# Row moves for the scan tables: three matmuls per pair of blocks, or three transfers and a mask

## The chip, the cores and the metric

The kernel runs on one core of one Trainium2 chip, in float32 arithmetic (TensorE works on numbers split into two parts). The metric is the device time of one execution in microseconds, lower is better, as a median of several runs.

## The reference

The program is a decoder trunk of two layers over 256 positions of width 2048. Layer 0 has a Mamba-2 branch and an attention branch in parallel, layer 1 is an S5 mixer, a diagonal complex state-space scan. The part that matters here is layer 1's scan:

```python
def s5_ssm(u, lam_re, lam_im, log_dt, b_re, b_im, c_re, c_im, d_skip):
    lam = lax.complex(lam_re, lam_im)                 # 128 groups x 64 states
    dt = jnp.exp(log_dt)[:, None]
    lam_bar = jnp.exp(lam * dt)
    b_bar = ((lam_bar - 1.0) / lam)[..., None] * lax.complex(b_re, b_im)
    c_mat = lax.complex(c_re, c_im)
    ...
        bu = jnp.einsum('gnm,blgm->blgn', b_bar, u_blk)
        ...
        _, hs = lax.associative_scan(_linear_recurrence, (a, bu), axis=1)
        y = jnp.einsum('gmn,blgn->blgm', c_mat, hs).real
    ...
    return y + d_skip * u

def reference(x, ...):
    for layer in range(2):
        h = ssd_moba_mixer(x, ...) if layer % 2 == 0 else s5_mixer(x, ...)
        x = layer_norm(alpha * x + h, ln_g[layer], ln_b[layer])
    return x
```

`s5_mixer` projects its input, runs `s5_ssm`, applies GELU and a GLU with a gate, and projects back.

## The kernel before

**The stream of weights.** All large products read weights in units of 128 partitions x 1024 float32 (512 KB). `split_to` loads a unit on SP's queue into one of four `raw` buffers, ScalarE rounds it to `wh` (L244) and VectorE takes the rest, `wl = raw - wh` (L249). `wh` and `wl` have four buffers each in the pool `st`. While TensorE works on one unit, `split_to(unit + 3)` has been written ahead. A product unit on TensorE is 12 matmuls of 512 columns: two halves of the unit, two row blocks of the output, and three terms (high x high, high x low, low x high; `xmm`, L293). `product_wide` orders the same work with the weights as the stationary side (L348, L349).

**Side work.** Everything else is written as small jobs. `pump` runs one or more of them after each unit: `jobs` are urgent, `back` is spread evenly up to a goal. `run` holds a job's instructions on ScalarE, VectorE and SP behind the splits of a unit two ahead. It does not hold POOL or TensorE.

**The order on each engine.** The program is built with `schedule_with_timeline_sim=True`: a planner decides, when the kernel is built, in which order each engine gets its instructions, from the times at which it expects their inputs to be ready. The code's order breaks ties. On the chip each engine then runs its own list strictly in that order and waits where an input isn't there. `tc.issue_after(x)` puts an instruction behind `x` on its engine.

**The tables of the S5 scan.** Layer 1 does its scan in steps of four positions, with tables for 16 blocks of eight groups each. The tables depend on the parameters alone, so they are made during layer 0, in the attention part, as `back` jobs, and stored in DRAM (`wb`, 1792 columns per block). Layer 1 loads them later (`wt`, L1273). For each block `block_jobs` makes:

- `bars` (L721), `efs`, `fcs`: factors on VectorE;
- `pes` (L765), once for each pair of an even and an odd block: four transposes for each block, stored with ScalarE's queue; 32 small matmuls (L780) whose result plus the skip term is `kt`, 128 rows x 128 columns (L782, L783). The rows come in groups of four, one group for each of 32 (group, channel) combinations, and the row inside a group is the lag;
- `mts` (L785), the step of the change, one job after the next block's `bars`: `om` gets four versions of `kt`. In version 3 - t the rows are moved up by t inside their group of four, and rows that would come from the next group are zero. Before the change, three matmuls with constant shift matrices (`shift`) do this on TensorE (L790), ScalarE copies each result out of PSUM (L794), and `om` is stored in two transfers on ScalarE's queue (L796).

After each block comes `phasors` (L695): 28 small operations on POOL and a store on POOL's own queue (L711). `phasor_job` holds it behind the last L934 written so far, POOL's one step of the attention part's rotary embedding; the transposes on TensorE need L934.

Of the kernel before, what the change touches and what calls it, by code (L numbers as in the profile page):

```python
# [9 lines left out]
F32 = mybir.dt.float32  # L10
# [38 lines left out]
def _fields(table, spec):  # L49
    at = 0  # L50
    for name, n in spec:
# [2 lines left out]
    return at  # L54


NCONST = _fields(CONST, [("ident", 128), ("causal", 256), ("tril", 128), ("shift", 384),
                         ("kmask", 16), ("sgn", 2), ("rope", 128), ("sel", 32)])
NPARAM = _fields(PARAM, [("convw", 96), ("convb", 24), ("normg", 16), ("ln0g", 16), ("ln0b", 16),
                         ("ssdd", 32), ("dtb", 1), ("alog", 1), ("s5d", 64)])  # L60
# [2 lines left out]
def _constants():  # L63
    c = np.zeros((P, NCONST), np.float32)

    def put(name, a):
        lo, hi = CONST[name]
        c[: a.shape[0], lo:hi] = a.reshape(a.shape[0], -1)

    i = np.arange(P)  # L70
    put("ident", np.eye(P, dtype=np.float32))
    causal = np.zeros((P, 256), np.float32)
    causal[:, 128:] = np.where(i[None, :] <= i[:, None], 0.0, NEG)
    put("causal", causal)
    put("tril", (i[None, :] >= i[:, None]).astype(np.float32))
    sh = np.zeros((P, 3, P), np.float32)
    for t in range(1, 4):
        for r in range(P):
            if r % 4 + t < 4:
                sh[r + t, t - 1, r] = 1.0  # L80
    put("shift", sh)
    put("kmask", ((i[:, None] % 4 == 3) & ((i[:, None] // 4) % 16 == np.arange(16)[None, :])).astype(np.float32))
    sg = np.where(i < 64, -1.0, 1.0).astype(np.float32)
    put("sgn", np.stack([sg, -sg], 1))
    inv = np.float32(500000.0) ** (-(np.arange(16, dtype=np.float32) * np.float32(2.0) / np.float32(32)))
    ang = np.arange(S, dtype=np.float32)[:, None] * inv[None, :].astype(np.float32)
    cos, sin = np.cos(ang).astype(np.float32).T, np.sin(ang).astype(np.float32).T
    put("rope", np.concatenate([cos, cos, -sin, sin], 0).T.reshape(2, P, 64).transpose(1, 0, 2))
    put("sel", np.tile(np.eye(32, dtype=np.float32), (2, 1)))
    return c  # L90
# [80 lines left out]
def trunk(tc, io, out):  # L171
# [8 lines left out]
    with ExitStack() as top:  # L180
# [274 lines left out]
        with ExitStack() as l0:  # L455
# [239 lines left out]
            def phasors(b):  # L695
# [14 lines left out]
                    n *= 2  # L710
                nc.gpsimd.dma_start(wb[b][:, 1280:1792].rearrange("p (a n) -> p a n", a=2), cs.rearrange("p a q c -> p a (q c)"))  # L711

            ktp = [None]
            pend = []
            late = []

            def block_jobs(b):
                h = {}
                gs = slice(8 * b, 8 * b + 8)

                def bars():  # L721
                    bc = h["bc"] = pp.tile([P, 4, 8, 16], F32, tag="bc", name=nm("bc"))
                    nc.sync.dma_start(bc.rearrange("p a g m -> p (a g m)"), io["s5bc"][b].rearrange("p a g m -> p (a g m)"))
                    bb = h["bb"] = pp.tile([P, 2, 8, 16], F32, tag="bb", name=nm("bb"))
                    cv = h["cv"] = pp.tile([P, 8, 16], F32, tag="cv", bufs=2, name=nm("cv"))
                    tm = pp.tile([P, 512], F32, tag="tm", name=nm("tm"))
                    tv = tm.rearrange("p (a g m) -> p a g m", a=4, g=8)
                    wr = wri[:, 0, gs].unsqueeze(2).to_broadcast([P, 8, 16])
                    wi = wri[:, 1, gs].unsqueeze(2).to_broadcast([P, 8, 16])
                    V.tensor_tensor(bb[:, 0], bc[:, 0], wr, op=OP.mult)  # L730
                    V.tensor_tensor(tv[:, 0], bc[:, 1], wi, op=OP.mult)
                    V.scalar_tensor_tensor(bb[:, 1], bc[:, 1], sgn, wr, op0=OP.mult, op1=OP.mult)
                    V.scalar_tensor_tensor(tv[:, 1], bc[:, 0], sgn, wi, op0=OP.mult, op1=OP.mult)
                    V.tensor_tensor(bb[:, 0], bb[:, 0], tv[:, 0], op=OP.add)
                    V.tensor_tensor(bb[:, 1], bb[:, 1], tv[:, 1], op=OP.subtract)
                    V.tensor_scalar(cv, bc[:, 2], nsg, None, op0=OP.mult)

                def lk(i, k):
                    return lam[:, i, gs, k - 1].unsqueeze(2).to_broadcast([P, 8, 16])

                def fk(i):
                    return lap[:, i, 4 * b : 4 * b + 4, :].unsqueeze(2).to_broadcast([P, 4, 16, 4])

                def efs():
                    bc, bb = h["bc"], h["bb"]
                    et = h["et"] = pp.tile([P, 8, 16, 4], F32, tag="et", bufs=2, name=nm("et"))
                    tm = pp.tile([P, 8, 16, 4], F32, tag="tm", name=nm("tm"))
                    for s in range(3):
                        V.tensor_tensor(et[:, :, :, s], bb[:, 0], lk(0, 3 - s), op=OP.mult)
                        V.tensor_tensor(tm[:, :, :, s], bb[:, 1], lk(1, 3 - s), op=OP.mult)  # L750
                    V.tensor_tensor(et[:, :, :, 0:3], et[:, :, :, 0:3], tm[:, :, :, 0:3], op=OP.add)
                    V.tensor_copy(et[:, :, :, 3], bb[:, 0])

                def fcs():
                    bc = h["bc"]
                    ob = h["ob"] = pp.tile([P, 1024], F32, tag="ob", bufs=2, name=nm("ob"))
                    cp = [bc[:, 3, 4 * i : 4 * i + 4, :].unsqueeze(3).to_broadcast([P, 4, 16, 4]) for i in range(2)]
                    for r in range(2):
                        fv = ob[:, 512 + 256 * r : 768 + 256 * r].rearrange("p (g m t) -> p g m t", g=4, m=16)
                        tm = pp.tile([P, 4, 16, 4], F32, tag="tm", name=nm("tm"))  # L760
                        V.tensor_tensor(fv, cp[0], fk(r), op=OP.mult)
                        V.tensor_tensor(tm, cp[1], fk(1 - r), op=OP.mult)
                        V.tensor_tensor(fv, fv, tm, op=OP.add if r else OP.subtract)

                def pes():  # L765
                    pair = [(b - 1, pend.pop()), (b, h)]
                    pk = aux()
                    kt = ktp[0] = pp.tile([P, 8, 16], F32, tag="kt", name=nm("kt"))
                    for n, (k, d) in enumerate(pair):
                        pe = aux()  # L770
                        ev = d["ev"] = d["et"].rearrange("p (a i) m s -> p a (i m s)", i=2)
                        transpose4(pe, [ev[:, a, :] for a in range(4)])
                        A.activation(d["ob"][:, 0:512], pe, AF.Copy)
                        nc.scalar.dma_start(wb[k][:, 0:1024], d["ob"])
                    for n, (k, d) in enumerate(pair):
                        cv = d["cv"].rearrange("p (a i) m -> p a i m", i=2)
                        for a in range(4):
                            for i in range(2):
                                at = 64 * (i ^ (a % 2))
                                T.matmul(pk[at : at + 64, 64 * n + a * 16 : 64 * n + a * 16 + 16], d["ev"][:, a, 64 * i : 64 * i + 64], cv[:, a, i, :], start=True, stop=True)  # L780
                    dc = PR("s5d")[:, 4 * b - 4 : 4 * b + 4].unsqueeze(2).to_broadcast([P, 8, 16])
                    V.tensor_tensor(kt, C("kmask").unsqueeze(1).to_broadcast([P, 8, 16]), dc, op=OP.mult)  # L782
                    V.tensor_tensor(kt, pk[:, 0:128].rearrange("p (a m) -> p a m", m=16), kt, op=OP.add)  # L783

                def mts():  # L785
                    kf = ktp[0].rearrange("p a m -> p (a m)")
                    pm = aux()
                    om = pp.tile([P, 512], F32, tag="om", name=nm("om"))
                    for j in range(3):
                        T.matmul(pm[:, j * 128 : j * 128 + 128], C("shift")[:, j * P : j * P + P], kf, start=True, stop=True)  # L790
                    mv = om.rearrange("p (k t) -> p t k", t=4)
                    V.tensor_copy(mv[:, 3, :], kf)
                    for j in range(3):
                        A.activation(mv[:, 2 - j, :], pm[:, j * 128 : j * 128 + 128], AF.Copy)  # L794
                    for i in range(2):
                        nc.scalar.dma_start(wb[b - 1 + i][:, 1024:1280], om[:, 256 * i : 256 * i + 256])  # L796

                if b % 2:
                    late.append(mts)
                    return [bars, efs, fcs, pes] + ([mts] if b == 15 else [])  # L800
                return [bars] + ([late[-1]] if late else []) + [efs, fcs, lambda: pend.append(h)]
# [733 lines left out]
```

## Time and profile before

| | |
|---|---|
| median of 3 runs | 1332.26 us (1331.92 to 1332.73) |
| the profiled execution, its own time | 1332.87 us |
| its span, first to last instruction | 1331.0 us |
| granted TensorE clock | 0.999 |
| busy: TensorE, VectorE, ScalarE, POOL | 99%, 72%, 52%, 25% |
| data moved | 282.73 MB, mean 212 GB/s |

The page names the engines PE (TensorE matmuls), PEld (its weight loads, which overlap), DVE (VectorE), ACT (ScalarE), POOL (GpSimd) and SP. A row of a timeline has the start in us, the length in us, engine, line, operation, output <- inputs, shapes, how often, and in brackets the idle time before it with what ended that. A row of a group has the same without the start, then the busy time and the mean length in ns, and the idle time before with its releasers. A row of the chain of waits has start, length and what ran. A DMA issue row gives the median time from issue to landing. The table blocks of layer 0 run between 400 and 800 us.

### The profile page before, as it was taken

To read this page: it belongs to the slowest core of one execution; us is meant where nothing else is said; L and a number is where in the kernel's file an instruction comes from. 1 tells how busy PE (TensorE), PEld (TensorE's weight loads), DVE (VectorE), ACT (ScalarE), POOL (GpSimd) and SP (SyncE) were. 2 spreads that over 40 slices of the span, in tenths; PEclk is the share of its full clock that TensorE was granted. 3 is DMA by queue.
4 is the path that set the end of the run, shared out by engine and by line. 5 is a ranking of instruction groups with operands and counts; after the bars stand their busy time and mean duration, and the time that the engine had idled before them with its cause. 6 is when DMAs were issued, how large, how long until landed. Compare 5 with 4: busy or idle time off the path is not lost.

```text
span 1331.0 us, 21530 instructions
## 1 busy us (share of the span) xinstructions
PE 1321.8 (99%) x8079; PEld 1111.5 (84%) x8079; DVE 961.6 (72%) x1612; ACT 692.8 (52%) x947; POOL 337.9 (25%) x646
## 2 busy tenths in 40 slices
PE   9999999999999999999999999999999999999998
PEld 8988888877888888888888888888888888888886
DVE  6778877775686777687797765858999846555565
ACT  5556668864644554554564434443445544444442
POOL 0043000121036625334787300023453100000000
PEclk9999999999999999999999999999999999999999
DMA  8555555444556657656757768469998675555762
GB/s 318 175 183 181 180 175 174 155 149 157 173 190 225 196 204 234 201 189 202 235 189 247 253 230 308 173 232 308 321 292 303 216 215 188 190 190 190 252 211 90
DMA packets 80732, 282.73 MB, mean 212 GB/s; under 512 B 9842, under 2 KB 12658, under 8 KB 80116
## 3 DMA queue, kind: packets, MB, share of 16 engines
q1 hardware_dynamic: 68260, 239.64, 54.4%
q0 software_dynamic: 7328, 30.42, 6.8%
q10 hardware_dynamic: 5040, 11.31, 2.4%
q8 instruction: 63, 1.03, 0.3%
q14 instruction: 41, 0.34, 0.1%
HBM read 260.35 MB, written 20.97 MB: 211 GB/s over the span
## 4 chain that ended last, share of the span: by engine, by line
PE 97%; DMA 2%; DVE 0%; ACT 0%; issue 0%; SPq 0%; ACTq 0%; POOLq 0%
PE main L293 61%; PE main L348 16%; PE main L349 8%; PE main L315 3%; PE aux L429 2%; DMA ud<-ut 1%; PE aux L872 1%; PE aux L780 1%; DMA um<-ud 1%; PE dec L1335 1%; PE aux L961 1%; PE enc L1290 1%; PE aux L993 1%; PE dec L1331 0%; PE aux L790 0%; PE aux L842 0%
## 5 line engine op out<-in xcount | busy, mean ns | idle before, releaser
L249 DVE TENSOR_TENSOR wl<-raw,wh 128x1024 fp32r<-128x1024 f32 x430 | 533.1, 1242 | 306.5 <-ACT wh L244 304.4
L244 ACT ACTIVATE wh<-raw 128x1024 fp32r<-128x1024 f32 x430 | 455.2, 1060 | 518.4 <-PE main L293 313.4
L293 PE MATMUL main<-wh,A 128*128 128x512 f32 x1536 | 490.0, 394 | 0.0
L293 PEld LDWEIGHTS main<-wh,A 128*128 128x128 f32 x1536 | 287.8, 188 | 59.2 <-issue 0.3
L293 PE MATMUL main<-wl,A 128*128 128x512 f32 x768 | 300.7, 392 | 0.0
L348 PE MATMUL main<-A,wh 128*128 128x512 f32 x768 | 273.1, 399 | 0.0
L293 PE MATMUL main<-wh,C 128*128 128x512 f32 x832 | 262.4, 393 | 0.3 <-ACT C L1110 0.3
L349 PE MATMUL main<-A,wl 128*128 128x256 f32 x768 | 215.3, 280 | 0.0
L293 PEld LDWEIGHTS main<-wh,C 128*128 128x128 f32 x832 | 155.6, 188 | 34.0 <-ACT C L1110 1.0
L348 PEld LDWEIGHTS main<-A,wh 128*128 128x128 f32 x768 | 144.2, 188 | 33.6
L293 PEld LDWEIGHTS main<-wl,A 128*128 128x128 f32 x768 | 144.3, 188 | 29.2 <-issue 0.5
L293 PE MATMUL main<-wl,C 128*128 128x512 f32 x416 | 162.5, 391 | 0.0
L349 PEld LDWEIGHTS main<-A,wl 128*128 128x128 f32 x768 | 145.1, 189 | 0.2
L706 POOL TENSOR_TENSOR c<-c 128x8 f32<-128x8 f32 (+2 forms) x192 | 97.3, 525 | 28.6 <-DMA wb<-c 21.0
L293 PEld LDWEIGHTS main<-wl,C 128*128 128x128 f32 x416 | 78.1, 188 | 16.2
L348 PE MATMUL main<-C,wh 128*128 128x512 f32 x192 | 68.2, 399 | 0.0
L934 POOL TENSOR_TENSOR b<-b 128x128 f32<-128x128 f32 x16 | 11.4, 710 | 194.5 <-DVE b L933 151.6
L881 POOL TENSOR_TENSOR ssq<-ssq,c 128x256 f32<-128x256 f32 x16 | 18.4, 1147 | 166.4 <-ACT c L879 165.9
L349 PE MATMUL main<-C,wl 128*128 128x256 f32 x192 | 53.6, 281 | 0.0
L708 POOL TENSOR_TENSOR c<-c,c 128x4 f32<-128x4 f32 (+2 forms) x96 | 46.5, 485 | 7.4
L709 POOL TENSOR_TENSOR c<-c,c 128x4 f32<-128x4 f32 (+2 forms) x96 | 45.7, 476 | 0.0
L315 PE MATMUL main<-A,wh 128*128 128x256 f32 x256 | 43.4, 284 | 1.4 <-ACT wh L236 1.4
(302 smaller groups left out, 1379.2 us busy)
## 6 DMA issues: line engine op xcount, KB each, us to landing
raw<-in_wi SPq DMA_DIRECT2D x270, 512.0 KB, 3.7
raw<-in_wo SPq DMA_DIRECT2D x96, 512.0 KB, 4.3
raw<-in_wglu SPq DMA_DIRECT2D x64, 512.0 KB, 3.3
wt<-wb POOLq DMA_DIRECT2D x16, 896.0 KB, 7.4
wb<-ob ACTq DMA_DIRECT2D x16, 512.0 KB, 5.1
bc<-in_s5bc SPq DMA_DIRECT2D x16, 256.0 KB, 3.8
wb<-c POOLq DMA_DIRECT2D x16, 256.0 KB, 3.8
wb<-om ACTq DMA_DIRECT2D x16, 128.0 KB, 3.3
```

Source lines behind the costliest of these rows:

```text
L244: high = A.activation(wh, raw, AF.Copy)
L249: splits[n] = (loaded[-1], high, V.tensor_tensor(wl, raw, wh.bitcast(F32), op=OP.subtract))
L293: end = T.matmul(ps[o], l[:, k, sl], r[:, j, :], start=start and i == 0, stop=stop and i == 2)
L315: T.matmul(pv[o // 2][:, o % 2, :], l[:, j, sl], r[:, k, :], start=first and i == 0 and o % 2 == 0, stop=end and i == 2 and o % 2 == 1, sk ...
L348: T.matmul(ps[o], wh[:, j, sl], xx[:, k, :, :].rearrange("p a n -> p (a n)"), start=first, stop=False, skip_group_check=True)
L349: T.matmul(ps[o][:, S : 2 * S], wl[:, j, sl], xh[:, k, :], start=False, stop=end, skip_group_check=True)
L429: end = T.transpose(dst[:, i * P : i * P + P], s, ident)
L706: G.tensor_tensor(p[:, :, :, 0:m], cs[:, :, :, 1 : m + 1], cs[:, i, :, n : n + 1].unsqueeze(1).to_broadcast([P, 2, 4, m]), op=OP.mult)
L708: G.tensor_tensor(cs[:, 0, :, n + 1 : n + 1 + m], p0[:, 0, :, 0:m], p1[:, 1, :, 0:m], op=OP.subtract)
L709: G.tensor_tensor(cs[:, 1, :, n + 1 : n + 1 + m], p0[:, 1, :, 0:m], p1[:, 0, :, 0:m], op=OP.add)
L780: T.matmul(pk[at : at + 64, 64 * n + a * 16 : 64 * n + a * 16 + 16], d["ev"][:, a, 64 * i : 64 * i + 64], cv[:, a, i, :], start=True, stop ...
L881: G.tensor_tensor(ssq, ssq, jk[:, f, :], op=OP.add)
```

## The change

The three shift matmuls go, and so does the constant `shift`. When `kt` is done, `pes` starts three transfers from SBUF to SBUF on POOL's queue: `kt` from row 1 + j on, into rows 0 to 126 - j of plane j of a new tile `moved` (127, 126 and 125 rows of 512 bytes). `mts` then copies each plane to `om` on ScalarE with a scale per row, which is one where the row's source lies in the same group of four and zero elsewhere (`inside`, three columns of constants). `moved` has one buffer, and it is cleared once on POOL, because the last rows of a plane are never written.

```diff
-NCONST = _fields(CONST, [("ident", 128), ("causal", 256), ("tril", 128), ("shift", 384),
+NCONST = _fields(CONST, [("ident", 128), ("causal", 256), ("tril", 128), ("inside", 3),
                          ("kmask", 16), ("sgn", 2), ("rope", 128), ("sel", 32)])
...
-    sh = np.zeros((P, 3, P), np.float32)
-    for t in range(1, 4):
-        for r in range(P):
-            if r % 4 + t < 4:
-                sh[r + t, t - 1, r] = 1.0
-    put("shift", sh)
+    put("inside", (i[:, None] % 4 + np.arange(1, 4)[None, :] < 4).astype(np.float32))
...
+            moved = pp.tile([P, 3, 128], F32, name="moved")
+            G.memset(moved, 0.0)
             ktp = [None]
...
                     kt = ktp[0] = pp.tile([P, 8, 16], F32, tag="kt", name=nm("kt"))
+                    kf = kt.rearrange("p a m -> p (a m)")
...
                     V.tensor_tensor(kt, pk[:, 0:128].rearrange("p (a m) -> p a m", m=16), kt, op=OP.add)
+                    for j in range(3):
+                        nc.gpsimd.dma_start(moved[0 : P - 1 - j, j, :], kf[1 + j : P, :])

                 def mts():
                     kf = ktp[0].rearrange("p a m -> p (a m)")
-                    pm = aux()
                     om = pp.tile([P, 512], F32, tag="om", name=nm("om"))
-                    for j in range(3):
-                        T.matmul(pm[:, j * 128 : j * 128 + 128], C("shift")[:, j * P : j * P + P], kf, start=True, stop=True)
                     mv = om.rearrange("p (k t) -> p t k", t=4)
                     V.tensor_copy(mv[:, 3, :], kf)
                     for j in range(3):
-                        A.activation(mv[:, 2 - j, :], pm[:, j * 128 : j * 128 + 128], AF.Copy)
+                        A.activation(mv[:, 2 - j, :], moved[:, j, :], AF.Copy, scale=C("inside")[:, j : j + 1])
```

## The prediction

> **What bounds the kernel now.** I read the page first, then the chain of waits, then the instructions of the lines that change, then the timelines of ACT and POOL around them.
>
> ```profile
> span 1331.0 us, 21530 instructions
> PE 1321.8 (99%) x8079; PEld 1111.5 (84%) x8079; DVE 961.6 (72%) x1612; ACT 692.8 (52%) x947; POOL 337.9 (25%) x646
> ...
> PE 97%; DMA 2%; DVE 0%; ACT 0%; issue 0%; SPq 0%; ACTq 0%; POOLq 0%
> ...
> L249 DVE TENSOR_TENSOR wl<-raw,wh 128x1024 fp32r<-128x1024 f32 x430 | 533.1, 1242 | 306.5 <-ACT wh L244 304.4
> L244 ACT ACTIVATE wh<-raw 128x1024 fp32r<-128x1024 f32 x430 | 455.2, 1060 | 518.4 <-PE main L293 313.4 <-PE main L348 98.8 <-issue 34.2
> ```
>
> TensorE is the bound: busy 99% of the span and 97% of the chain that ended last. ACT makes `wh` of each weight unit (L244) and mostly waits for PE to free one of four buffers; DVE makes `wl` after it (L249). So whatever PE sheds shortens the run, as long as ACT and DVE stay ahead. The table blocks run between 400 and 800 us, and there PE never rests. The three matmuls that go are on the chain:
>
> ```profile
> 597.33 0.67 PE aux L790 x6
> 598.00 2.77 PE main L293 x12
> ```
>
> ```profile
> L790 PE MATMUL aux<-kt,consts x48: 270/275/275, 433.2 to 797.9; 128*128 128x128 f32 x48
> ```
>
> **What goes.** Each pair of blocks issues three float32 matmuls, recorded as six passes: 48 for eight pairs. Their busy spans overlap (48 x 0.274 = 13.2 us would count them twice); on the chain six passes take 0.67 us. Eight pairs: 8 x 0.67 = 5.36 us. Nothing else on PE waits for them, so this is the whole gain: span 1331.0 to 1325.6. The profiled execution took 1332.87 us and the median of the runs is 1332.26, so I carry the difference over to the median: 1332.26 - 5.36 = 1326.9.
>
> **What has one answer.** The three L794 activations stay, with a per-row scale and an SBUF source; ACT has 518 us of idle before L244, and a change of some hundredths of a microsecond in 24 instructions is nothing. One PSUM buffer less is taken per pair. The consts load shrinks from 1074 to 693 columns, early on; PE idles 9.2 us in the whole run (1331.0 - 1321.8), so at most a fraction of a microsecond comes of it. One POOL memset is added, once, while POOL idles.
>
> **What is added: three transfers per pair on POOL's queue, and a wait on ACT.** The three moves wait for `kt` (L783), and ACT's L794 waits for all three to land. Behind L794 on ACT stand the `wh` splits, for which DVE and then PE wait. So the question is how long ACT may stand. The tightest pairs are those of blocks 10-11, with 5.1 us from `kt` to L794, and 14-15:
>
> ```profile
> 702.56 0.29 DVE L783 TENSOR_TENSOR kt<-aux,kt 128x128 f32<-128x128 f32 x1 [0.18 <-PE aux L780]
> ...
> 705.03 1.06 ACT L244 ACTIVATE wh<-raw 128x1024 fp32r<-128x1024 f32 x1 [2.34 <-PE main L293]
> 707.97 0.86 ACT L794 ACTIVATE om<-aux 128x128 f32<-128x128 f32 x3 [1.88 <-PE aux L790]
> 708.62 1.06 ACT L244 ACTIVATE wh<-raw 128x1024 fp32r<-128x1024 f32 x1
> ```
>
> ```profile
> 792.81 0.28 DVE L783 TENSOR_TENSOR kt<-aux,kt 128x128 f32<-128x128 f32 x1
> ...
> 795.24 1.06 ACT L244 ACTIVATE wh<-raw 128x1024 fp32r<-128x1024 f32 x1 [2.63 <-PE main L293]
> ```
>
> The split at 705.03 began when PE freed a buffer, that is at the start of a unit; a unit is 12 matmuls, 2.77 us (the chain row above). The split behind L794 is for the unit that PE starts four units later: 705.03 + 4 x 2.77 = 716.1. Before that it needs L244 and L249 (1.06 + 1.24 = 2.30) and the three L794 (0.86). So the moves may land until **712.95**, 10.1 us after `kt` (702.85). For blocks 14-15 the same working gives 803.2, 10.1 us after 793.09. The other pairs leave more room. What lands later is lost by PE one for one.
>
> The price of a transfer on this queue, from the phasor store, its nearest relative (128 rows, written to DRAM):
>
> ```profile
> L711 POOL DMA_DIRECT2D wb<-c x16: 585/585/773, 403.9 to 747.4; - x16
> ...
>   POOL c L706: 21.0, 10
> ...
> DMA to landing us min/median/max: 2.3/3.8/5.5
> ```
>
> Three issues of 0.585 us one after another, the last landing 3.8 us after its start: 2 x 0.585 + 3.8 = **5.0 us** from the moment POOL reaches the moves (3.5 to 6.7 with the ends of the row). From `kt` that is 707.9, before L794's own place. If POOL reaches them when `kt` is done, all is hidden.
>
> **When does POOL reach them?** Each engine runs its instructions in a fixed order, planned at build time (`schedule_with_timeline_sim=True`) by expected times: an instruction goes where the planner thinks its inputs are ready. POOL's other work here is the phasors, 28 small operations and a store per block. They need nothing from PE and are held only behind the last L934, so POOL runs far ahead with them. All eight left after 616 us run without a break:
>
> ```profile
> 616.01 0.10 POOL L698 MEMSET c<- 128x4 f32 x1
> ...
> 747.45 0.58 POOL L711 DMA_DIRECT2D wb<-c  x1 [0.30 <-POOL c L709]
> ```
>
> (748.0 - 616.0) / 8 = 16.5 us each on the chip. When `kt` of blocks 10-11 is done, 86.9 us after 616.0, the chip is in the sixth of the eight. If the planner reckons p us per phasor, it puts the moves behind 86.9 / p phasors, and the chip comes there at T = 616.0 + 86.9 x 16.5 / p, at the latest 748.0. With p = 16.5 that is 702.9 and costs nothing; with a smaller p the moves stand behind phasors that the chip has yet to do. Two readings of p:
>
> ```profile
> 586.17 0.10 POOL L698 MEMSET c<- 128x4 f32 x1
> ...
> 587.09 1.09 POOL L708 TENSOR_TENSOR c<-c,c 128x4 f32<-128x4 f32 x1
> 588.13 0.21 POOL L709 TENSOR_TENSOR c<-c,c 128x4 f32<-128x4 f32 x1
> ...
> 589.75 0.46 POOL L934 TENSOR_TENSOR b<-b 128x128 f32<-128x128 f32 x1
> ...
> 597.31 0.58 POOL L711 DMA_DIRECT2D wb<-c  x1 [0.30 <-POOL c L709]
> ```
>
> ```profile
> 588.36 0.21 DVE L933 TENSOR_TENSOR b<-main,consts 128x64 f32<-128x64 f32 x1
> ```
>
> First, this least disturbed phasor: 597.89 - 586.17 = 11.7 us, less the L934 inside it (0.46) and one blocked operation (L708 took 1.09 where its like takes 0.21: 0.88), 10.4; plus 2.1 for the wait on the store before it (21.0 us in 10 waits) gives 12.5. Second, that L934 stands inside the phasor, so the planner placed it by its readiness. On the chip its input (L933) was done at 588.57, but POOL came to it at 589.75: it needed 3.58 us where the planner allowed about 2.40. A ratio of 1.49 makes p = 16.5 / 1.49 = 11.1. I take the middle, **p = 11.8**: T = 616.0 + 121.5 = 737.5, landing 742.5, PE loses 742.5 - 712.95 = 29.6 us. Net +29.6 - 5.36 = +24.2: **1356.5 us**. The slow end is the whole phasor with its blocks, 11.7 + 2.1 = 13.8: T = 719.9, landing 724.9, loss 12.0, net +6.6, 1338.9. The fast end is a planner that has all phasors done: T = 748.0, landing 753.0, loss 40.1, net +34.7, 1367.0.
>
> Why only this pair: the one before it falls among the first two of the eight phasors.
>
> ```profile
> 637.61 0.28 DVE L783 TENSOR_TENSOR kt<-aux,kt 128x128 f32<-128x128 f32 x1
> ...
> 649.75 0.86 ACT L794 ACTIVATE om<-aux 128x128 f32<-128x128 f32 x3
> ```
>
> Here POOL would be at most 2 x (16.5 - 11.8) = 9.4 us late; 637.9 + 9.4 + 5.0 = 652.3, and with the 5 us of room behind L794 that the other pair has (712.95 - 707.97) it is hidden. Earlier phasors start right behind an L934 and have drifted less, later pairs find POOL done. Behind the moves on POOL wait only phasors, which are read in the next layer, so POOL standing for `kt` costs nothing.
>
> [...]
>
> **The rivals.** *A, hidden (the other sign):* the planner reckons with phasors as slow as the chip's, or slower. Then POOL reaches the moves with `kt`, or waits for it, ACT does not stand, and the whole 5.36 us is won: **1326.9 us** (at most 13.2 / 2 = 6.6 us, if two passes overlap throughout, 1325.6). It decides from p of about 15.2 up: there T + 5.0 = 715.3 loses 2.4 us. For it speaks that the planner's times are not in the trace and that one L934 is a thin sample; against it, the 1.49.
>
> *C, slow landing:* A's order, but a move of 127 rows lands late because few DMA engines share it. Small packets, while the weights run (an answer for 798 to 804 us, with the 1 KB rows of `om` on q10):
>
> ```profile
> q1 hardware_dynamic: 294, 1.13, 59.5%
> q10 hardware_dynamic: 288, 0.26, 12.6%
> ```
>
> 0.126 x 16 x 6 us / 288 = 0.042 us a packet. On one engine 127 rows take 5.3 us alone, and 5.3 / (1 - 0.595) = 13.2 if the weights keep their share: 9.1 to 17.0 us from issue to landing. Against 10.1 us of room in two pairs that loses 0 to 2 x 6.9 = 13.8 us; in the middle, 13.0, it loses 5.8 and cancels the gain: **1332.7 us** (1326.9 to 1340.7). For it: the odd row count. Against it: the 64-row transfers here show no such thing, and nothing in the trace has 127 rows. [...]
>
> **How the numbers follow.** The forecast, moves stuck behind phasors, 0.50; A 0.35; C 0.15. A difference under 0.2%, 2.7 us, can hardly be told from no change. Faster: A 0.35 and 0.04 of C, 0.39. Same: 0.06 of C and 0.01 of the forecast, 0.07. Slower: 0.49 and 0.05, 0.54. Both signs hold much, so the range spans them: 1325.6 (A's low end) to 1367.0 (the forecast's high end); the forecast's own is 1338.9 to 1367.0.
>
> **What would show it.** L790 is gone in every case. If the forecast is right, POOL's timeline has the three moves of blocks 10-11 behind L711s after 716 us, ACT's waits list L794 for a DMA or POOL with one wait of 20 to 40 us near 710, PE has one gap there, and the rest of the chain is unchanged. If A is right, PE stays at 99%, L794's waits are under 10 us, and the span falls by 5.4 us. If C is right, the moves are issued at `kt` and land 10 to 17 us later, and PE shows gaps of a few us in two pairs. I would be wrong altogether if PE's new idle time lay outside 400 to 800 us, or if L934, waiting behind a move, made the transposes late.

## The result and the profile after

The changed kernel is slower: **1350.4 us** median of 4 runs (1349.33 to 1355.52), against 1332.49 us for the kernel before on the same chip; ratio 1.0142, 95% interval 1.0129 to 1.0154. The forecast of 1356.5 us had the sign and the mechanism, and was 6.1 us too high. The lines of the code have moved: L706 is now the phasor store (L711 before), L239 and L244 the splits (L244, L249), L288 the product (L293), L781 the end of `kt` (L783), L783 the moves, L791 ACT's masking copies into `om` (L794).

The page of the kernel after: span, busy times, TensorE's busy tenths and granted clock in 40 slices, and the chain.

```profile
span 1348.4 us, 21476 instructions
PE 1320.0 (98%) x8031; PEld 1108.5 (82%) x8031; DVE 961.0 (71%) x1612; ACT 695.3 (52%) x947; POOL 340.8 (25%) x671
PE   9999999999999999999994999999999999999998
PEclk9999999999999999999996999999999999999999
PE 89%; POOL 6%; DMA 2%; issue 1%; ACT 0%; DVE 0%; SPq 0%; POOLq 0%; ACTq 0%; DVEq 0%
```

One slice in forty is bad, the one from 708 to 742 us, and there the clock falls too. POOL, which was not on the chain before, now holds 6% of it. The waits of the kernel after (who <- for whom: total, times, longest, in us) name the links:

```profile
PE main L288 <- ACT wh L239: 19.2, 1, 19.2
...
ACT om L791 <- DMA moved<-kt: 33.4, 4, 27.3
```

PE waits once, 19.2 us, for a split on ACT; ACT has one wait of 27.3 us for the moves. The timelines of DVE, POOL, ACT and PE for that stretch, in this order:

```profile
699.22 0.29 DVE L781 TENSOR_TENSOR kt<-aux,kt 128x128 f32<-128x128 f32 x1 [0.18 <-PE aux L778]
...
707.86 0.59 POOL L706 DMA_DIRECT2D wb<-c  x1 [0.30 <-POOL c L704]
...
718.05 0.59 POOL L706 DMA_DIRECT2D wb<-c  x1 [0.30 <-POOL c L704]
...
727.88 1.62 POOL L783 DMA_DIRECT2D moved<-kt  x3
729.49 0.58 POOL L706 DMA_DIRECT2D wb<-c  x1
```

```profile
701.70 1.06 ACT L239 ACTIVATE wh<-raw 128x1024 fp32r<-128x1024 f32 x1 [2.34 <-PE main L288]
730.06 0.82 ACT L791 ACTIVATE om<-moved,consts 128x128 f32<-128x128 f32 x2 [27.30 <-DMA moved<-kt]
730.68 1.05 ACT L239 ACTIVATE wh<-raw 128x1024 fp32r<-128x1024 f32 x1
```

```profile
712.15 0.39 PE L288 MATMUL main<-wh,C 128*128 128x512 f32 x1
731.78 0.80 PE L288 MATMUL main<-wh,C 128*128 128x512 f32 x1 [19.24 <-ACT wh L239]
```

`kt` of blocks 10-11 is done at 699.5. POOL issues its three moves at 727.9, with all of the eight phasors' arithmetic ahead of them and only the last store behind. ACT stands meanwhile at L791, and with it the splits; PE uses up its split units and stops at 712.5. The moves themselves land 2.2 us after POOL has begun to issue them.

The stretches of the kernel after (length in us, then busy us and instructions of PE, PEld, DVE, ACT, POOL, then granted clock, DMA share, GB/s) show a second loss behind the gap:

```profile
720.00:725.00 5.00, 0.00 (x0) 0.00 (x0) 0.00 (x0) 0.00 (x0) 3.96 (x17) 0.50 0.00 0
...
730.00:735.00 5.00, 2.75 (x6) 1.86 (x7) 3.24 (x9) 4.00 (x6) 0.07 (x1) 0.50 0.54 185
735.00:740.00 5.00, 5.00 (x18) 3.98 (x17) 5.00 (x9) 2.10 (x3) 0.00 (x0) 0.75 0.40 146
740.00:745.00 5.00, 5.00 (x24) 4.05 (x23) 4.97 (x8) 2.13 (x2) 0.00 (x0) 1.00 0.62 209
```

PE is back at 731.8, but at half clock until about 737.5. What the whole costs is read from `kt` of the next pair, blocks 12-13, in DVE's timeline before and after:

```profile
743.53 0.28 DVE L783 TENSOR_TENSOR kt<-aux,kt 128x128 f32<-128x128 f32 x1
```

```profile
762.12 0.28 DVE L781 TENSOR_TENSOR kt<-aux,kt 128x128 f32<-128x128 f32 x1
```

For blocks 10-11 the change was 3.34 us ahead (702.85 against 699.51), which is five pairs by 0.67. One pair later it is 18.59 us behind. The swing of 21.9 us, with the 0.67 that the sixth pair saves, is a loss of 22.6: 19.2 of idle, 0.5 behind it (PE's next wait, for `wl`), and 2.6 to 2.9 for the slow clock (half of the 5.7 us at half speed, without or with the 0.5 of waiting in them). The two pairs left save 1.34, so 17.3 us should remain at the end: the span grew by 17.4.

### The profile page after: what moved, and what is told of

Its sections match the earlier page's. It is cut to its first block, busy times and chain, and to the rows that moved or that the text cites. A ratio compares the mean times of both kernels' runs of the same rounds, so it can differ in the third digit from the quotient of the medians.

```text
span 1348.4 us, 21476 instructions
## 1 busy us (share of the span) xinstructions
PE 1320.0 (98%) x8031; PEld 1108.5 (82%) x8031; DVE 961.0 (71%) x1612; ACT 695.3 (52%) x947; POOL 340.8 (25%) x671
## 4 chain that ended last, share of the span: by engine, by line
PE 89%; POOL 6%; DMA 2%; issue 1%; ACT 0%; DVE 0%; SPq 0%; POOLq 0%; ACTq 0%; DVEq 0%
PE main L288 55%; PE main L343 16%; PE main L344 8%; POOL c L701 3%; PE main L310 3%; DMA wb<-c 2%; PE aux L424 2%; POOL c L703 1%; POOL c L704 1%; PE aux L869 1%; PE enc L1287 1%; PE dec L1332 1%; DMA raw<-in_wi 1%; PE dec L1328 0%; PE aux L778 0%
## 5 line engine op out<-in xcount | busy, mean ns | idle before, releaser
L244 DVE TENSOR_TENSOR wl<-raw,wh 128x1024 fp32r<-128x1024 f32 x430 | 532.9, 1243 | 321.7 <-ACT wh L239 318.0
L239 ACT ACTIVATE wh<-raw 128x1024 fp32r<-128x1024 f32 x430 | 455.5, 1061 | 495.9 <-PE main L288 302.6
L288 PE MATMUL main<-wh,A 128*128 128x512 f32 x1536 | 489.6, 394 | 0.0
L288 PEld LDWEIGHTS main<-wh,A 128*128 128x128 f32 x1536 | 287.8, 188 | 59.2 <-issue 0.3
L288 PE MATMUL main<-wl,A 128*128 128x512 f32 x768 | 300.6, 391 | 0.0
L288 PE MATMUL main<-wh,C 128*128 128x512 f32 x832 | 263.9, 395 | 19.6 <-ACT wh L239 19.2
L288 PEld LDWEIGHTS main<-wh,C 128*128 128x128 f32 x832 | 156.7, 189 | 54.0 <-ACT wh L239 19.7
L288 PEld LDWEIGHTS main<-wl,A 128*128 128x128 f32 x768 | 144.3, 188 | 29.3 <-issue 0.5
L288 PE MATMUL main<-wl,C 128*128 128x512 f32 x416 | 163.5, 393 | 0.5 <-DVE wl L244 0.5
L701 POOL TENSOR_TENSOR c<-c 128x8 f32<-128x8 f32 (+2 forms) x192 | 95.7, 517 | 19.9 <-DMA wb<-c 12.4
L288 PEld LDWEIGHTS main<-wl,C 128*128 128x128 f32 x416 | 78.6, 189 | 17.3 <-DVE wl L244 1.0
L878 POOL TENSOR_TENSOR ssq<-ssq,c 128x256 f32<-128x256 f32 x16 | 18.4, 1147 | 166.4 <-ACT c L876 165.8
L703 POOL TENSOR_TENSOR c<-c,c 128x4 f32<-128x4 f32 (+2 forms) x96 | 40.9, 426 | 7.4
L343 PEld LDWEIGHTS main<-C,wh 128*128 128x128 f32 x192 | 35.8, 188 | 8.2
```

The lines of the kernel that those rows point to most:

```text
L239: high = A.activation(wh, raw, AF.Copy)
L244: splits[n] = (loaded[-1], high, V.tensor_tensor(wl, raw, wh.bitcast(F32), op=OP.subtract))
L288: end = T.matmul(ps[o], l[:, k, sl], r[:, j, :], start=start and i == 0, stop=stop and i == 2)
L343: T.matmul(ps[o], wh[:, j, sl], xx[:, k, :, :].rearrange("p a n -> p (a n)"), start=first, stop=False, skip_group_check=True)
L701: G.tensor_tensor(p[:, :, :, 0:m], cs[:, :, :, 1 : m + 1], cs[:, i, :, n : n + 1].unsqueeze(1).to_broadcast([P, 2, 4, m]), op=OP.mult)
L703: G.tensor_tensor(cs[:, 0, :, n + 1 : n + 1 + m], p0[:, 0, :, 0:m], p1[:, 1, :, 0:m], op=OP.subtract)
```

## The experiments

Two theories. **Order:** the moves of blocks 10-11 stand on POOL behind phasors that the chip has not done, and nothing else of the change costs anything. **Transfers:** the moves are slow, or disturb the stream of weights. Every time below stands beside the kernel before on the same chip.

**e1, every phasor behind the moves written before it.**

```diff
-                    with tc.issue_after(turns[-1].ins):
+                    with ExitStack() as pin:
+                        pin.enter_context(tc.issue_after(turns[-1].ins))
+                        if moves:
+                            pin.enter_context(tc.issue_after(moves[-1].ins))
                         phasors(b)
```

> Edit: the phasors of every block are held behind the moves that were written before them, on POOL; transfers, their queue and all else stay. Theory 1 (the moves of blocks 10-11 stand behind phasors that the chip has not yet done; POOL's order is the whole loss): POOL now waits for kt instead, ACT's wait at L791 for blocks 10-11 falls from 27 us to under 5, TensorE's 19 us gap and the slow clock behind it vanish, and the 5.4 us of the removed matmuls show: 1327 us, within 1 us. Theory 2 (the transfers themselves land late): the order changes nothing about landing, ACT still waits 10 us or more in two or more pairs: 1332 us or above. Theory 3 (waiting on POOL is harmful in itself, through a late rotary step L931): gaps before transposes, above 1330 us.

Measured: 1331.93 us (10 runs), ratio 0.9991 (0.9981 to 1.0000). The 19 us gap is gone, and ACT waits 5.5 us in all:

```profile
ACT om L795 <- DMA moved<-kt: 5.5, 4, 2.2
```

Order is confirmed as the cause of the loss, but the time is some 5 us above the expected 1327, and most of the 5.4 us of gain is missing. The number fits the third theory, but its mechanism does not show: PE waits nowhere for POOL. The gain is there as far as blocks 14-15 (`kt` at 786.9 us, 5.9 ahead of before) and goes in the layer norm between the layers, where PE's transposes wait for DVE. The stretch before, and the stretch and the two PE rows of e1:

```profile
840.00:860.00 20.00, 20.00 (x102) 16.64 (x101) 17.66 (x30) 6.70 (x11) 0.00 (x0) 1.00 0.49 176
```

```profile
840.00:860.00 20.00, 17.73 (x82) 14.41 (x83) 16.91 (x27) 7.42 (x12) 0.00 (x0) 0.91 0.35 125
...
841.48 0.66 PE L424 MATMUL aux<-consts,D 128*128 128x128 f32 x4 [1.86 <-DVE D L1102]
842.93 0.66 PE L424 MATMUL aux<-consts,D 128*128 128x128 f32 x4 [0.79 <-DVE D L1102]
```

2.3 us idle and 20 us at a mean clock of 0.91 (up to 1.8 us): up to 4.1 us, which is about the missing gain. DVE's layer norm stands there behind splits whose weights came late: before 825.5 us ACT waits 3.4 us for a load, in e2 0.2 us at that place. Why the loads are late in e1 was not settled. In e2, e6 and e10 PE idles at most 0.2 us in that stretch; in e11 0.6 us, in e9 1.4 us (both below).

**e2, the moves on SP's queue.**

```diff
-                        nc.gpsimd.dma_start(moved[0 : P - 1 - j, j, :], kf[1 + j : P, :])
+                        nc.sync.dma_start(moved[0 : P - 1 - j, j, :], kf[1 + j : P, :])
```

> Edit: the three moves per pair are issued on SP's queue, where the weight loads are, instead of POOL's. Theory 1 (POOL's order): no phasor stands ahead of them, so no 27 us wait; about 1327 us, if SP waiting for kt does not delay weight loads by more than the three units that are loaded ahead; a late load would show as ACT waiting for raw. Theory 2 (127 rows land late): on this queue too; with one DMA engine for 127 rows 5 to 13 us from issue to landing, then ACT waits of up to 8 us in the tight pairs, 1327 to 1335 us.

Measured: **1328.28 us** (1328.2 to 1328.74, 4 runs), ratio 0.9960 (0.9945 to 0.9975), span 1326.4. It beats the kernel before by 4.65 us in the medians. The ratio makes 5.3 us of it, and its interval, 3.3 to 7.3 us, holds the whole gain of 5.36. The waits and timelines of e2 show that the moves are slower here than on POOL's queue:

```profile
ACT om L791 <- DMA moved<-kt: 14.4, 5, 5.2
```

```profile
699.14 6.87 SPq L783 DMA_DIRECT2D moved<-kt  x3
...
709.39 1.25 ACT L791 ACTIVATE om<-moved,consts 128x128 f32<-128x128 f32 x3 [4.32 <-DMA moved<-kt]
```

Some 10 us pass from the first issue to ACT's start, 6.9 of them until SP has issued the third move, against 2.2 us in all on POOL's queue. ACT's room of 10 us hides it.

**e3, the reading step later.** `mts` goes one pair on, behind the next odd block's `fcs`; moves on POOL as in the change.

```diff
+                    before = [late[-1]] if late else []
                     late.append(mts)
-                    return [bars, efs, fcs, pes] + ([mts] if b == 15 else [])
-                return [bars] + ([late[-1]] if late else []) + [efs, fcs, lambda: pend.append(h)]
+                    return [bars, efs, fcs] + before + [pes] + ([mts] if b == 15 else [])
+                return [bars, efs, fcs, lambda: pend.append(h)]
```

> Edit: mts runs one pair later, just before the next pes, so ACT comes to the moved rows some 40 us after kt instead of some 5 to 15; the moves keep their queue and, for blocks 10-11, stand even behind the last phasor. Theory 1: POOL comes to them some 40 us after kt as before, but ACT now comes no earlier, so the wait is gone or a few us: 1327 to 1332 us. Theory 2 (slow landing): also hidden, so the same; this run tells only whether the loss is the wait of ACT or something else that the moves do, in which case it stays at 1340 to 1350 us.

Measured: 1334.16 us (10 runs), ratio 1.0009 (0.9999 to 1.0018). The planner put the moves of 10-11 further back still, behind the last phasor store, so ACT's later read still had to wait for them:

```profile
739.20 1.59 POOL L783 DMA_DIRECT2D moved<-kt  x3 [0.26 <-issue]
...
742.25 1.10 ACT L791 ACTIVATE om<-moved,consts 128x128 f32<-128x128 f32 x3 [12.02 <-DMA moved<-kt]
```

Giving ACT more time takes away nearly all of the loss, but the gain does not come: the moves were issued 11.3 us later than in the change, and used the new time up. PE still idles 2.9 us behind them, and from 745 to 750 us the mean clock is 0.66. The time lies between the ranges of the two theories. A later reader is no cure where the order is planned anew around it.

**e4, the transfers alone.** The kernel before, its matmuls kept, with three transfers per pair beside them that nobody reads (448-byte rows).

```diff
+                    for j in range(3):
+                        nc.gpsimd.dma_start(moved[0 : P - 1 - j, j, :], kf[1 + j : P, 0:112])
```

> Edit on the kernel before: the matmuls stay and om is filled from them; the transfers are issued beside them on POOL's queue into a tile that nobody reads (rows of 448 bytes instead of 512, for lack of space). It prices the transfers and POOL's waiting alone. Theory 1: nobody waits for them, so 1332.3 us, within 1 us, though POOL comes to the moves of blocks 10-11 late again; the only waiter is the next pair's kt (it must not overwrite rows not yet read), more than 10 us of room. If the transfers or POOL's waits disturb the weights or the rotary step, above 1334 us.

Measured: 1332.73 us (10 runs), ratio 0.9997 (0.9987 to 1.0006). POOL comes to the moves of blocks 10-11 late here too (L788 in e4), behind the same phasors:

```profile
743.67 1.62 POOL L788 DMA_DIRECT2D moved<-kt  x3
```

The next pair's `kt` has to wait for them and is 6 us later than before (749.5 against 743.5), but PE does not wait for it. Transfers that ACT does not wait for cost nothing measurable. The theory that they disturb the weights falls.

**e5, e6, e7: how many phasors stand ahead of the moves of blocks 10-11.** The last one, two or four phasors are held behind these moves (`HOLD` is `(15,)`, `(14, 15)`, `(12, 13, 14, 15)`).

```diff
+                        if b in HOLD:
+                            pin.enter_context(tc.issue_after(moves[11].ins))
                         phasors(b)
```

> Edit on the changed kernel: only the phasor of block 15 is held behind the moves of blocks 10-11, so on POOL they stand one phasor earlier than in the changed kernel. Theory 1 (the loss is the time at which POOL reaches these moves): one undisturbed phasor is 10.2 us in the changed kernel's trace while ACT and DVE stood (L706 at 707.86 to 718.05), so ACT's wait of 27.3 us falls to about 17, TensorE's gap of 19.2 to about 9, and with a little less slow clock the time from 1350 to about 1339. Theory 2 (something else in the moves): no such step.

> Edit on the changed kernel: the phasors of blocks 14 and 15 are held behind the moves of blocks 10-11, two phasors earlier than in the changed kernel. Theory 1: POOL reaches the moves about 20 us sooner, ACT's wait is about 7 us, within the room behind L791, TensorE has no gap or one under 1 us: 1327 to 1330 us. Theory 2: no such step.

> Edit on the changed kernel: the phasors of blocks 12 to 15 are held behind the moves of blocks 10-11, so POOL waits for kt instead of being late. Theory 1: ACT's wait is under 3 us for this pair, no gap; 1327 us, or up to 1332 if the gap of some 2.6 us that the first order test showed in the layer norm comes back, which would then belong to the shifted timing there and not to the moves.

Rows of POOL and ACT for blocks 10-11 in e5, in e6 and in e7 (there L788 are the moves, L798 ACT's copies); the last two rows of e7 are blocks 12-13:

```profile
718.05 1.59 POOL L788 DMA_DIRECT2D moved<-kt  x3
...
720.24 0.97 ACT L798 ACTIVATE om<-moved,consts 128x128 f32<-128x128 f32 x2 [18.37 <-DMA moved<-kt]
```

```profile
708.52 1.59 POOL L788 DMA_DIRECT2D moved<-kt  x3
...
710.70 0.94 ACT L798 ACTIVATE om<-moved,consts 128x128 f32<-128x128 f32 x2 [8.46 <-DMA moved<-kt]
```

```profile
699.26 1.59 POOL L788 DMA_DIRECT2D moved<-kt  x3 [21.61 <-ACT C L1005]
...
705.11 1.01 ACT L798 ACTIVATE om<-moved,consts 128x128 f32<-128x128 f32 x2 [3.16 <-DMA moved<-kt]
...
754.83 1.67 POOL L788 DMA_DIRECT2D moved<-kt  x3
...
756.87 1.49 ACT L798 ACTIVATE om<-moved,consts 128x128 f32<-128x128 f32 x3 [9.20 <-DMA moved<-kt]
```

| phasors held | moves issued, us | ACT's wait | PE's gap | time, us | ratio (95%) |
|---|---|---|---|---|---|
| none (the change) | 727.9 | 27.3 | 19.2 | 1350.4 | 1.0142 (1.0129, 1.0154) |
| one (e5) | 718.05 | 18.4 | 10.5 | 1340.4 | 1.0058 (1.0041, 1.0074) |
| two (e6) | 708.5 | 8.5 | 2.5 (three waits) | 1330.8 | 0.9985 (0.9976, 0.9994) |
| four (e7) | 699.3 | 3.2 | none here | 1332.5 | 0.9999 (0.9989, 1.0008) |

Each of the first two phasors taken from ahead of the moves is worth 9 to 10 us of ACT's wait, 8 to 9 of PE's gap and 10 of the time. This shows the order theory and its price. e6 ended just above what was expected, and e7 missed: held phasors run later, so the moves of blocks 12-13 now stand behind them (754.8) and take over the wait. PE idles 2.0 us between 740 and 760. That is the theory again, one pair on. The trace is of the shortest of e7's ten executions (1331.15 us); what the others lost beyond this it does not show.

**e8, blocks 10-11 back to matmuls.** Seven pairs use the moves; this pair makes its shifted rows on TensorE from a widened identity, with the same mask on ACT.

```diff
-                    for j in range(3):
+                    for j in range(3 if b != 11 else 0):
                         nc.gpsimd.dma_start(moved[0 : P - 1 - j, j, :], kf[1 + j : P, :])
...
+                    if b == 11:
+                        pm = aux()
+                        for j in range(3):
+                            T.matmul(pm[:, j * 128 : j * 128 + 128], C("ident")[:, j + 1 : j + 1 + P], kf, start=True, stop=True)
```

> Edit on the changed kernel: blocks 10-11 alone go back to three matmuls (with shifted slices of a widened identity and the mask on ACT), the other seven pairs keep their transfers, POOL's order is as planned. Theory 1 (this pair alone makes the loss): no 27 us wait and no gap; 7 x 0.67 = 4.7 us are won: 1327.6 us, up to 1330 if the layer norm's gap shows. Rival (the transfers cost something in every pair): 1340 us or more remain.

Measured: 1329.47 us (10 runs), ratio 0.9977 (0.9968 to 0.9987). With this one pair back on TensorE the loss is gone, and the seven others bring 3.1 us of their 4.7.

**e9, e10, e11: what is left on SP's queue.** e9 cuts each move into 112 rows and the rest:

```diff
-                        nc.gpsimd.dma_start(moved[0 : P - 1 - j, j, :], kf[1 + j : P, :])
+                        nc.sync.dma_start(moved[0:112, j, :], kf[1 + j : 113 + j, :])
+                        nc.sync.dma_start(moved[112 : P - 1 - j, j, :], kf[113 + j : P, :])
```

> The moves on SP's queue, each in two pieces: 112 rows and the remaining 15, 14 or 13. With the whole moves on SP's queue, ACT stood 14.4 us in 5 waits for them, and in blocks 10-11 some 10 us passed from the first issue to the last landing, against 3.6 us on POOL's queue. If the odd number of 127, 126 or 125 rows makes that slow (few DMA engines share a move), the pieces of 112 rows land in 4 to 5 us and ACT's waits fall to under 6 us in all. If SP's queue itself is slow there (the 512 KB loads of weights ahead of the moves on the same queue), six transfers instead of three make it no better: ACT's waits stay at 12 to 20 us in all. Either way most of it is hidden by ACT's room of 10 us: 1327 to 1330 us.

e10 joins the edits of e2 and e3:

> The moves on SP's queue, and ACT's read of them some 12 us later, behind the table products of the next block. If what is left of the cost of SP's queue is ACT's wait for the landing (14.4 us in all, at most 5.2), it goes to zero and the time is that of the full gain, 1326.5 to 1327.5 us. If ACT's waits were hidden already and what is left is SP's own delay (6.9 us of issue ahead of a load of weights), or the read at its new place holds up other work, the time stays at 1328 us or rises by one to two.

e11 puts the moves of one pair on SP:

```diff
-                        nc.gpsimd.dma_start(moved[0 : P - 1 - j, j, :], kf[1 + j : P, :])
+                        (nc.sync if b == 11 else nc.gpsimd).dma_start(moved[0 : P - 1 - j, j, :], kf[1 + j : P, :])
```

> The changed kernel, with the moves of blocks 10-11 alone issued on SP; the other seven pairs stay on POOL's queue behind the phasors as planned. By the theory that this one pair, standing behind phasors, makes the whole loss, the 27 us wait of ACT falls to about 5 us, the gap of PE of 19 us goes, and the time is 1327 to 1329 us, like the moves all on SP. If POOL's order harms other pairs as well, or the 5.4 us are given back elsewhere, it stays above 1331 us.

Measured: e9 1329.75 us (8 runs), ratio 0.9974 (0.9964 to 0.9984); e10 1328.17 (5 runs), 0.9964 (0.9951 to 0.9978); e11 1329.61 (9 runs), 0.9974 (0.9964 to 0.9983). ACT's waits for the moves in e9:

```profile
ACT om L792 <- DMA moved<-kt: 5.6, 5, 2.3
```

14.4 us became 5.6 with twice as many transfers, as expected if the row count made the whole moves slow. The packet records of the traces show how: for blocks 10-11 the packets of the whole moves in e2 run from 704.4 to 709.7 us, in the last microsecond 42 packets one after another, while the pieces of e9 are through at 707.6. The time did not follow (e2 and e10, with more and with almost no waiting of ACT, are equal), so ACT's waits on SP's queue were hidden, as e10 was to show. SP still takes 6.9 us until the six pieces of blocks 10-11 are issued, and in e2 the first packet comes 5.2 us after SP's first issue, so the row count is not all of it. e11 confirms e8 from the other side: only one pair was moved away from POOL, and the loss is gone. Its 1329.6 is just above the 1327 to 1329 expected, with ACT's longest wait at 6.2 us. The best versions are e2 and e10, which no run here tells apart; e2 differs from the change by one word.

## Why the prediction came out as it did

**The bound and the gain: right.** PE is the bound, and a pair saves 0.67 us, shown by the lead of 3.34 us after five pairs. Rival A's 1326.9 us is about what one gets where nothing stands behind phasors: e2's ratio makes 0.9960 x 1332.26 = 1326.9 (1324.9 to 1328.9), its median 1332.26 - 4.65 = 1327.6.

**The mechanism: right, by each of its signs.** L783 behind L706 stores after 716 us, one wait of 20 to 40 us at L791 (27.3), one gap of PE, the rest as it was. Only this pair: e8 and e11. The sentence that POOL may stand for `kt` at no cost holds for the change, but not for an order that is pushed around (e7).

**The size: 6.1 us too much, because of one term, T.** It was put at 737.5 and was 727.9, which alone is 9.6 us too much; the slow clock, left out of the sum, makes up for some 3 us of that. T had two factors, and both were off:

- The planner's pace p was taken as 11.8 us. The moves stand behind nearly eight phasors, 86.2 us from POOL's start on them (613.3) to `kt`: p is about 10.8, an estimate that takes the planner's time to `kt` to be the chip's. The moves of blocks 8-9, behind two phasors with `kt` 21.9 us after that start, give much the same. By this alone T would be 613.3 + 86.2 x 16.5 / 10.8 = 745.0, further off.
- The chip's pace was taken as 16.5 us throughout. The first six phasors took 15.9 us each (613.30 to 708.44, with 1.6 us of issue for the moves of blocks 8-9; DVE is busy 74.7 us of these 95.1), the seventh 10.2. The row that carries it is the stretch of the seventh, in the kernel after:

```profile
707.86:718.05 10.19, 4.68 (x21) 3.55 (x19) 0.00 (x0) 0.00 (x0) 7.86 (x30) 0.95 0.07 27
```

DVE is busy 0.00 us in it: ACT stood, no `wh` came, so DVE had no `wl` to make, and POOL ran undisturbed. The jam sped up the very work that it was waiting for. A constant pace, read from a stretch in which DVE was busy, could not hold in a stretch in which the forecast itself had stopped DVE. e4 bears this out: there ACT does not wait, DVE goes on, and in the same order POOL reaches the moves at 743.67, 15.8 us later than in the change.

**Small terms.** With the measured T the forecast's own rule gives 727.9 + 5.0 - 712.95 = 19.9 us of idle (19.2 and 0.5 measured). Its parts were off and cancelled, which is luck: the moves landed in 2.2 us instead of 5.0, PE ran out 3.6 us earlier than by the timeline of before (it was 3.3 us ahead), and it needed 1 us less from the landing on (ACT makes the split before its third copy, and PE starts with `wh` alone). The slow clock was not in the sum. In the kernel after the granted clock went to 0.50 at 717.0 us, 4.5 us after PE's last matmul ended (712.5), and back to 1.00 at 737.5, 5.7 us after PE's next one began (731.8); with PE at work it cost 2.6 to 2.9 us. In sum, 1326.9 + 19.7 + 2.9 = 1349.5, against 1350.4.

**Rival C: refuted for the queue in question.** On POOL's queue the moves of 127, 126 and 125 rows land like the phasor store, which takes 3.4 us there (the DMA issues of the kernel after, KB each, median us to landing):

```profile
moved<-kt POOLq DMA_DIRECT2D x8, 63.5 KB, 3.7
moved<-kt POOLq DMA_DIRECT2D x8, 63.0 KB, 3.5
moved<-kt POOLq DMA_DIRECT2D x8, 62.5 KB, 3.2
```

The pages' counts of packets (queue, kind: packets, MB, share of 16 engines) show how the two queues differ. These are POOL's queue, q0, before and after, and SP's queue, q1, before and in e2:

```profile
q0 software_dynamic: 7328, 30.42, 6.8%
q0 software_dynamic: 8096, 31.97, 7.1%
```

```profile
q1 hardware_dynamic: 68260, 239.64, 54.4%
q1 hardware_dynamic: 71444, 240.99, 52.7%
```

On POOL's queue a pair adds 96 packets. By their sizes in the trace, each move is 16 packets of up to eight rows and 16 of four bytes. In blocks 10-11 the 16 large ones of the first move begin within 0.21 us (729.03 to 729.24) and take 0.16 to 0.24 us each. On SP's queue a pair adds 398: 378 packets of one row and 20 of four bytes. Rival C's sum has all 127 rows on one engine, 5.3 us; no run shows how many engines share a move. At the 42 rows in a microsecond seen in e2, 127 rows one after another take about 3.0 us, an estimate.

## What to carry to other kernels

Before a transfer is put on an engine's queue, ask what that engine will have been given ahead of it in the fixed order: a planner that takes an engine to be half as fast again as it is parks the transfer behind work that isn't done, and whoever reads the transfer pays. Put it on a queue that keeps pace with its producer, even one on which it lands later, as long as the reader's room covers that: here SP's 10 us were free and POOL's 2.2 us cost 18. And when a forecast stops an engine, work out the pace of the others again without it.

## What the runs showed of the hardware

POOL's phasor takes 10.2 us while DVE rests and 14 to 21 us beside DVE's splits. It is single operations that grow. In the kernel after, between 400 and 760 us, the 72 operations of L701 that meet no DVE instruction take 0.62 us at most, those beside a two-input operation of DVE up to 1.64. In the kernel before one of L709 took 3.44 us while DVE ran five such operations in a row. The rows show two of 128x8 in the kernel before, beside a split of DVE that runs from 616.48 for 1.23 us, and one of the same in the kernel after while DVE rested:

```profile
616.48 1.46 POOL L706 TENSOR_TENSOR c<-c 128x8 f32<-128x8 f32 x2
```

```profile
708.92 0.21 POOL L701 TENSOR_TENSOR c<-c 128x8 f32<-128x8 f32 x1
```

Short gaps of PE can cost more than their length: in e1 2.3 us of idle came with a mean clock of 0.91 over 20 us, up to 1.8 us more. They need not: in e6 2.5 us of idle in three gaps came with a clock of 1.00.
